# Layer 0's later modulations, moved from the chain stage to beneath the projection stage of a two-layer hybrid backbone

## Chip, cores and metric

One core of a Trainium2 chip. The metric is the time of one execution on the device in microseconds (us); for the kernel before it is the median of three runs. The engines are TensorE (PE; its weight loads are a row of their own, PEld), VectorE (DVE), ScalarE (ACT), GpSimd (POOL) and SyncE (SP), which only issues DMAs.

## What is computed

Two layers over 512 latent and 256 context tokens of width 1024, in fp32. Each sub-layer is norm, modulate, mixer, norm, gate, residual; the modulations are six vectors per layer, made from the conditioning vector by one large matrix:

```python
def ada_mod(cvec, w, b):
    m = jax.nn.silu(cvec) @ w + b            # (1024) @ (1024 x 6144)
    return six pieces of 1024                # shift, scale, gate; shift, scale, gate

for layer in range(2):
    ml, mc = ada_mod(c, ...), ada_mod(c_ctx, ...)
    hl = modulate(rmsnorm(xl), ml[0], ml[1]); hc = modulate(rmsnorm(xc), mc[0], mc[1])
    # layer 0: [spatial-gating MLP, 4 groups | bidirectional RWKV-7, 8 heads];  layer 1: mLSTM
    yl, yc = mixer(hl, hc)                   # layer 0: p = h @ w_in ... concat(...) @ w_out
    xl = xl + ml[2] * rmsnorm(yl)
    hl = modulate(rmsnorm(xl), ml[3], ml[4])
    xl = xl + ml[5] * rmsnorm(conv_ffn(hl))  # the same for the context with mc
```

Layer 0 needs pieces 0 and 1 before the projection, pieces 2 to 4 only after its mixer's output projection.

## The kernel before

All weights of the large products are split into a high and a low part, and each product is three matmuls (high by high, high by low, low by high). What matters here are two stages of layer 0.

**Projection stage** (about 60 to 372 us). `unit(col)` makes one tile of 128 output channels of `h @ w_in`: SP loads 512 KB into a buffer `raw_win` (line 115), ACT makes the high part (`hi_win`, line 124), POOL the low part (`lo_win`, line 125), and PE runs 24 matmuls over the 512 latent tokens (`pl_...`, lines 266 to 268) and 24 over the 256 context tokens (`pc_...`). There are two buffers each for raw, high and low, in the pool `wkR`. Three kinds of jobs use the results:
- `kr(ct)` and `v(ct)` make the tiles `kT`, `rT` and `vT` of RWKV's channel tile `ct` (0 to 3), with a convolution of three taps on ACT and DVE.
- `prep_e`, `prep_n` and `prep_t` prepare channel tile `ct` for the chains: small products from the low-rank inputs (`zw`, `za`, lines 504 to 506), the sets `RB` and `LB`, products of 64 x 64 (`nx`, `ny`, lines 565 and 566), and a blockwise triangular inverse whose steps go from PE (`w`, line 621, `t`, line 630) to DVE (`Td`, line 604) and ACT (`TT`, lines 613 and 614) and back. `Ts[0]` and `Ts[1]` are the inverses of channel tiles 2 and 3. The sets are stored to DRAM by SP (`setd`, lines 550 and 577).
- `sgu(g)` is spatial gate `g` (0 to 3): `unit` for `u`, `unit` for `v` (`vg`, ACT, line 813), and then in two parts (2 and 4 chunks of 128 tokens) transposes on PE (`vt`, line 822), a norm (`vn`), the product (`pz`, line 833) and its use on DVE.

Python generators hold these jobs, and `weave` merges them into one order: each entry is (generator, number of steps, offset), and at each step that generator goes on whose share of steps done is smallest, the share running from its offset to 1. `part_of(g, n)` runs n steps of a generator and leaves the rest. The tile scheduler keeps this order roughly and moves instructions by its own rules. `bank(name, "67")` takes the PSUM banks 6 and 7 in turn.

**Chain stage** (372 to about 616 us). The recurrences run in blocks b = 0 to 5 as chains (`c`, `y`, lines 708 to 743), woven with the preparation of the next block's operands (`lt`, line 653; `vt`, line 657; `az`, line 668; lines 621 and 630 still for `Ts`), and with the finished outputs. In blocks 2 to 4 the products of modulations 2 to 4 are woven in:

```python
            if b == 0:
                todo.append((chained(Ts[0], part_of(Ts[1], 6)), 14))
            elif b == 1:
                todo.append((inverse(), 9))
            elif b < 5:
                todo.append((part_of(ada, (5, 6, 5)[b - 2]), (5, 6, 5)[b - 2]))
```

`ada_gen(g, ...)` computes modulations 2 and 3 (g = 1) and 4 (g = 2). Over eight pieces of the contraction SP loads a slab of the matrix (line 154), and PE multiplies it with the two conditioning vectors; four 512-column pieces go to four 32-column quadrants of one bank (line 157, `32x512`). At the end there is a copy (`adasb`, line 162), four transposes (`adat`, line 165), and two sums into `mod`. In this kernel the slab has 2048 columns (1 MB) for g = 1 and 1024 (512 KB) for g = 2, in two buffers of the pool `late0`. Their first use is at the end of block 4.

Of the kernel before, what the change touches and what calls it, by code (L numbers as in the profile page):

```python
# [74 lines left out]
def _build(ctx, tc, xall, par, cst, ada_0, ada_w, ada_t, w_in, w_out, ffn_up, ffn_down, lora, wsT, a_bs, c_in, c_gate, c_out, mneg, parf, parm, out):  # L75
# [9 lines left out]
    def bank(name, role):  # L85

        turn[role] = turn.get(role, -1) + 1
        return pp.tile([P, 512], F32, tag=role[turn[role] % len(role)], name=name)
# [55 lines left out]
    def ada_gen(g, pool, tag, rawb, cols=1024, rtag="araw", width=None):  # L144

        n = min(2048, 5120 - g * 2048)
        width, cols = width or cols, min(cols, n)
        m = n // 512
        pb = bank(f"ada_{g}", tag)
        for kt in range(KT):  # L150
            for c0 in range(0, n, cols):
                pl = pool[(c0 // cols) % len(pool)] if isinstance(pool, list) else pool
                raw = pl.tile([P, width], F32, tag=rtag, name=f"ada{g}{kt}{c0}", bufs=rawb)[:, :cols]
                nc.sync.dma_start(raw, ada_w[kt, :, (g - 1) * 2048 + c0:(g - 1) * 2048 + c0 + cols])
                for q2 in range(cols // 512):
                    q = c0 // 512 + q2
                    nc.tensor.matmul(pb[32 * q:32 * q + 32, :], silu[:, kt, :],
                                     raw[:, q2 * 512:(q2 + 1) * 512],
                                     start=(kt == 0), stop=(kt == KT - 1))
            yield  # L160
        sb = (pool[0] if isinstance(pool, list) else pool).tile([P, width], F32, tag=rtag, name=f"adasb_{g}", bufs=rawb)[:, :512]
        V.tensor_copy(sb[:32 * m], pb[:32 * m])
        pt = bank(f"adat_{g}", tag)
        for j in range(4):
            nc.tensor.transpose(pt[:, j * 128:j * 128 + 32 * m], sb[:32 * m, j * 128:(j + 1) * 128], ident[:32 * m, :32 * m])

        o = PC.at["ada_b0"][0]
        for cnd in range(2):
            V.tensor_tensor(mod[0][:, cnd, g * 16:g * 16 + 4 * m].rearrange("p (q j) -> p q j", q=m),
                            pt.rearrange("p (j q r) -> p q j r", j=4, q=4)[:, :m, :, cnd],  # L170
                            par_s[:, o + g * 16:o + g * 16 + 4 * m].rearrange("p (q j) -> p q j", q=m), ALU.add)
# [130 lines left out]
    def weave(*gens):  # L302
        for _ in woven(*gens):
            pass

    def part_of(g, n):
        for _ in range(n):
            next(g)
            yield

    def run(gen):
        for _ in gen:
            pass
# [16 lines left out]
    with ExitStack() as lx:  # L330
# [471 lines left out]
                yield  # L802

        def sgu(g):
            role = "7" if g == 3 else "67"
            pl, pcx = unit(g, f"u{g}")
            ug = wkR.tile([P, T], F32, tag="ug", name=f"ug{g}", bufs=1)
            A.activation(ug[:, 0:TC], pcx, AF.Gelu_apprx_tanh)
            A.activation(ug[:, TC:T], pl, AF.Gelu_apprx_tanh)
            yield  # L810
            pl, pcx = unit(4 + g, f"vg{g}")
            vg = wkR.tile([P, T], F32, tag="vg", name=f"vg{g}", bufs=1)
            A.activation(vg[:, 0:TC], pcx, AF.Gelu_apprx_tanh)
            A.activation(vg[:, TC:T], pl, AF.Gelu_apprx_tanh)
            bsb = wkR.tile([P, P], F32, tag="bsb", name=f"bsb{g}")
            nc.sync.dma_start(bsb, a_bs[:, g * 128:g * 128 + 128].to_broadcast([P, P]))
            yield
            for (t0, nt) in ((0, 2), (2, 4)):
                pt = bank(f"vt{g}{t0}", role)
                for i in range(nt):  # L820
                    tk = t0 + i
                    nc.tensor.transpose(pt[:, i * 128:i * 128 + 128], vg[:, tk * 128:tk * 128 + 128], ident)
                ss = sm.tile([P, 4], F32, tag="ss4", name=f"sgss{g}{t0}", bufs=2)
                vn = wkR.tile([P, 512], F32, tag="vn", name=f"vn{g}{t0}", bufs=1)
                for i in range(nt):
                    A.activation(vn[:, i * 128:i * 128 + 128], pt[:, i * 128:i * 128 + 128], AF.Square, accum_out=ss[:, i:i + 1])
                G.tensor_scalar(ss[:, :nt], ss[:, :nt], 1.0 / 128, EPS, ALU.mult, ALU.add)
                G.tensor_tensor(ss[:, :nt], ss[:, :nt], eps_t[:, 2:3].to_broadcast([P, nt]), ALU.pow)
                V.tensor_tensor(vn[:, :nt * 128].rearrange("p (a q) -> p a q", q=128), pt[:, :nt * 128].rearrange("p (a q) -> p a q", q=128),
                                ss[:, :nt].unsqueeze(2).to_broadcast([P, nt, 128]), ALU.mult)  # L830
                pz = bank(f"pz{g}{t0}", role)
                for i in range(nt):
                    mm(pz[:, i * 128:i * 128 + 128], vn[:, i * 128:i * 128 + 128], wsT_s[:, g * 128:g * 128 + 128], start=True, stop=True)
                w = nt * 128
                o = vg[:, t0 * 128:t0 * 128 + w]
                ugs = ug[:, t0 * 128:t0 * 128 + w]
                V.scalar_tensor_tensor(o.rearrange("p (a q) -> p a q", q=128),
                                       pz[:, 0:w].rearrange("p (a q) -> p a q", q=128), pc("a_gv", g),
                                       bsb.unsqueeze(1).to_broadcast([P, nt, 128]),
                                       ALU.mult, ALU.add)  # L840
                V.tensor_tensor(o, o, ugs, ALU.mult)
                yield
            nc.sync.dma_start(mixd[g], vg)
# [15 lines left out]
        def chained(*gens):  # L859
            for g in gens:  # L860
                yield from g

        def start_prep(ct):
            PLt = keep.tile([P, 24], F32, name=f"PL{ct}")
            st[ct]["PL"] = PLt
            for k, n in SET:
                if k not in ("vT", "TT"):
                    st[ct][k] = wkS.tile([P, n], F32, tag=k, name=f"{k}{ct}")
            return prep_e(ct, st[ct]["kT"], st[ct]["rT"])
# [13 lines left out]
                yield  # L883

        NA = (4, 6, 6)
        Ts = [prep_t(ct, lambda name: bank(name, "7")) for ct in (2, 3)]
        run(kr(0))
        weave((start_prep(0), 8), (chained(v(0), kr(1), part(0)), 3 + 0))
        run(prep_n(0))
        for ct in range(3):  # L890
            n = NA[ct]
            weave((prep_t(ct, prbank), 13, 0.0) if ct < 2 else (part_of(Ts[0], 7), 7, 0.2), (chained(start_prep(ct + 1), prep_n(ct + 1)), 9 + 3, 0.0),
                  (chained(v(ct + 1), *([kr(ct + 2)] if ct < 2 else []), part(n)), 3 + n, 0.0))
        run(SG)
        ex.close()
        hx.close()
        rx.close()
# [49 lines left out]
            nc.sync.dma_start(t, set_part(ct, "bv"))  # L947
            st[ct]["bv"] = t

        late = {}  # L950

        def inverse():
            yield from Ts[1]
            tx.close()
            late["p"] = lx.enter_context(tc.tile_pool(name="late0", bufs=1))
            nc.scalar.dma_start(lwg, lora[:, 1024:1536])

        def preps(cts, g):
# [14 lines left out]
        for b, (k, g) in enumerate(blocks):  # L973
            n = (22, 20, 22 - 10 * k)[g]
            todo = [(part_of(C[k], n) if g < 2 or k else C[k], n)]
            if b < 5:
                kk_, gg_ = blocks[b + 1]
                todo.append((preps(pairs[kk_], gg_), 10))
            if b == 0:
                todo.append((chained(Ts[0], part_of(Ts[1], 6)), 14))  # L980
            elif b == 1:
                todo.append((inverse(), 9))
            elif b < 5:
                todo.append((part_of(ada, (5, 6, 5)[b - 2]), (5, 6, 5)[b - 2]))
            if b == 3:
                for ct in range(2):
                    load_bv(ct)
                todo.append((finish((0, 1), ys[0], ("01", "01"), "ctx"), 8))
            elif b == 4:
                todo.append((finish((0, 1), ys[0], ("01", "01"), "lat"), 8))  # L990
            elif b == 5:
                todo.append((finish((2, 3), ys[1], ("01", "01"), "ctx"), 8))
            weave(*todo)
            if g < 2:
                run(part_of(C[k], 4))
            if b == 1:
                ada = ada_job([1, 2], late["p"], 2, 2048)
            if b == 2:
                C.append(chains(pairs[1], ys[1]))
            if b == 4:  # L1000
                run(ada)
                gate_rows(0, 0, "7")
                scale_vec(0, 1)
                load_bv(2)
                load_bv(3)
# [606 lines left out]
```

## Time and profile before

| | us |
|---|---|
| median of 3 runs | 1954.63 (1948.76 to 1961.74) |
| the profiled execution | 1946.71 |
| its span, first to last instruction | 1944.9 |
| TensorE busy (12411 matmuls) | 1825.8 |
| VectorE busy | 1332.6 |
| ScalarE busy | 800.8 |
| GpSimd busy | 305.7 |
| mean granted TensorE clock | 0.97 of full |

Busy times are shares of one execution by the hardware profiler, and an engine's idle time is listed with what released it. The profiled execution is 0.4% below the median of the timed runs. Times within it, such as "372", are us from the start of its span.

### The profile page before, as it was taken

How to read it: one execution, taken by the hardware profiler on the slowest of the kernel's cores; microseconds unless marked ns; L12 is line 12 of the kernel's file. 1: busy time of each engine (PE TensorE's matmuls, PEld its weight loads, DVE VectorE, ACT ScalarE, POOL GpSimd, SP SyncE). 2: the span in 40 equal slices, each digit the busy share in tenths (PEclk: the TensorE clock that was granted, in tenths of full speed). 3: DMA queues.
4: the chain of work that ended last, by engine and by line, in shares of the span. 5: the costliest groups of instructions: out<-in, count | busy, mean ns of one | idle time of the engine just before them, and what ended most of it. 6: DMA issues, size and time to landing. Idle time of an engine off the chain costs nothing.

```text
span 1944.9 us, 31874 instructions
## 1 busy us (share of the span) xinstructions
PE 1825.8 (94%) x12411; PEld 1501.0 (77%) x12411; DVE 1332.6 (69%) x2669; ACT 800.8 (41%) x1429; POOL 305.7 (16%) x429
## 2 busy tenths in 40 slices
PE   6998789698998999999999998999999989999998
PEld 4777677587756888888888887778888768888886
DVE  4379676857445589999994337667777678777534
ACT  4374645524335542222232226575554343333322
POOL 2222222311000222323330002100110010000001
PEclk9999889889998999999999999999999999999999
DMA  7133121633774534444432224421111312222222
GB/s 296 55 125 125 67 96 65 194 83 93 221 201 137 173 106 158 152 168 163 163 136 77 101 96 163 159 86 44 33 44 44 130 68 98 97 96 95 93 97 87
DMA packets 102887, 227.77 MB, mean 117 GB/s; under 512 B 28224, under 2 KB 44048, under 8 KB 99664
## 3 DMA queue, kind: packets, MB, share of 16 engines
q1 hardware_dynamic: 100976, 222.26, 33.8%
q10 hardware_dynamic: 1760, 3.47, 0.5%
q8 instruction: 98, 1.61, 0.3%
q14 instruction: 53, 0.43, 0.1%
HBM read 199.31 MB, written 26.39 MB: 116 GB/s over the span
## 4 chain that ended last, share of the span: by engine, by line
PE 58%; DVE 2%; ACT 2%; POOL 1%; issue 1%; POOLq 0%; DVEq 0%; ACTq 0%
PE of L1044 5%; PE of L1045 5%; PE of L1043 5%; PE pl_fb L267 4%; PE pl_fb L268 4%; PE pl_fb L266 4%; PE pl_fa L267 4%; PE pl_fa L266 4%; PE pl_fa L268 4%; PE pd L1456 1%; PE pe L1433 1%; PE pc_fb L268 1%; PE pc_fa L268 1%; PE pc_fb L267 1%; PE pc_fa L267 1%; PE pc_fb L266 1%
## 5 line engine op out<-in xcount | busy, mean ns | idle before, releaser
L1091 DVE SCALAR_TENSOR_TENSOR cv<-pl_fa,fpar,cv 128x441 f32<-128x441 f32 (+2 forms) x352 | 243.2, 691 | 15.3 <-ACT cv L1080 10.0
L1045 PE MATMUL of<-hi_fd,hlo 128*128 128x512 f32 x440 | 171.4, 392 | 3.1 <-DVE hlo L1115 3.1
L1044 PE MATMUL of<-lo_fd,hhi 128*128 128x512 f32 x440 | 172.1, 391 | 1.6 <-DVE lo_fd L125 1.6
L1043 PE MATMUL of<-hi_fd,hhi 128*128 128x512 f32 x440 | 171.1, 391 | 0.0
L201 DVE SCALAR_TENSOR_TENSOR aj<-am,srb 128x512 f32<-128x512 f32 x224 | 163.4, 730 | 6.3 <-DMA am<-in_ada_t_dram 1.1
L1115 DVE TENSOR_TENSOR hlo<-hid,hhi 128x512 fp32r<-128x512 f32 (+1 forms) x66 | 39.1, 601 | 128.5 <-ACT hhi L1114 128.3
L1114 ACT ACTIVATE hhi<-hid 128x512 fp32r<-128x512 f32 (+1 forms) x66 | 36.7, 559 | 170.6 <-PE of L1044 167.2
L1045 PEld LDWEIGHTS of<-hi_fd,hlo 128*128 128x128 f32 x440 | 83.2, 189 | 20.7 <-DVE hlo L1115 3.5
L1044 PEld LDWEIGHTS of<-lo_fd,hhi 128*128 128x128 f32 x440 | 82.7, 188 | 19.9 <-DVE lo_fd L125 3.1
L125 DVE TENSOR_TENSOR lo_fd<-raw_fd,hi_fd 128x1024 fp32r<-128x1024 f32 x66 | 80.8, 1224 | 25.0 <-ACT hi_fd L124 24.9
L1043 PEld LDWEIGHTS of<-hi_fd,hhi 128*128 128x128 f32 x440 | 82.8, 188 | 17.9 <-DVE pt_f L1028 0.4
L222 POOL TENSOR_SCALAR rstd_p_f<-sq_f,sq_f 128x1 f32<-128x1 f32 x10 | 7.2, 724 | 557.2 <-ACT jk_f L1022 557.2
L124 ACT ACTIVATE hi_fd<-raw_fd 128x1024 fp32r<-128x1024 f32 x66 | 69.3, 1049 | 27.9 <-DMA raw_fd<-in_ffn_down_dram 11.8
L124 ACT ACTIVATE hi_fa<-raw_fa 128x1024 fp32r<-128x1024 f32 x44 | 46.4, 1055 | 76.3 <-PE pl_fb L267 62.7
L124 ACT ACTIVATE hi_fb<-raw_fb 128x1024 fp32r<-128x1024 f32 x44 | 46.7, 1062 | 68.2 <-PE pc_fa L267 39.0
L125 POOL TENSOR_TENSOR lo_fb<-raw_fb,hi_fb 128x1024 fp32r<-128x1024 f32 x22 | 59.4, 2698 | 88.9 <-ACT hi_fb L124 88.9
L125 POOL TENSOR_TENSOR lo_win<-raw_win,hi_win 128x1024 fp32r<-128x1024 f32 x23 | 57.6, 2508 | 91.2 <-ACT hi_win L124 85.0
L1093 ACT ACTIVATE cv<-cv 128x512 f32<-128x512 f32 x44 | 27.8, 632 | 106.4 <-DVE cv L1091 106.4
L266 PE MATMUL pl_fa<-h0f_lathi,hi_fa 128*128 128x512 f32 x176 | 69.0, 392 | 0.0
L266 PE MATMUL pl_fb<-h0f_lathi,hi_fb 128*128 128x512 f32 x176 | 68.8, 391 | 0.0
L267 PE MATMUL pl_fb<-h0f_latlo,hi_fb 128*128 128x512 f32 x176 | 68.8, 391 | 0.0
L267 PE MATMUL pl_fa<-h0f_latlo,hi_fa 128*128 128x512 f32 x176 | 68.8, 391 | 0.0
(695 smaller groups left out, 5485.5 us busy)
## 6 DMA issues: line engine op xcount, KB each, us to landing
raw_fd<-in_ffn_down_dram SPq DMA_DIRECT2D x66, 512.0 KB, 3.2
am<-in_ada_t_dram SPq DMA_DIRECT2D x112, 256.0 KB, 2.9
raw_fa<-in_ffn_up_dram SPq DMA_DIRECT2D x44, 512.0 KB, 3.3
raw_fb<-in_ffn_up_dram SPq DMA_DIRECT2D x44, 512.0 KB, 3.2
raw_win<-in_w_in_dram SPq DMA_DIRECT2D x23, 512.0 KB, 3.3
ada<-in_ada_dram SPq DMA_DIRECT2D x8, 1024.0 KB, 8.8
ada<-in_ada_w_dram SPq DMA_DIRECT2D x8, 1024.0 KB, 7.0
raw_cin<-in_c_in_dram SPq DMA_DIRECT2D x16, 512.0 KB, 3.5
```

The source lines that it names most:

```text
L124: nc.scalar.activation(hi[:, c], raw[:, c], AF.Copy)
L125: strm.sub.tensor_tensor(lo[:, c], raw[:, c], hi[:, c].bitcast(F32), ALU.subtract)
L201: V.scalar_tensor_tensor(place(f"aj{i}{h}{cnd}", "junk"), raw, 1.0, sb[cnd * 2 + h], ALU.mult, ALU.mult, accum_out=acc[:, cnd, h:h + 1])
L266: mm(p, wh[:, kt, :], hh[:, kt], start=(kt == 0), stop=False)
L267: mm(p, wh[:, kt, :], hl[:, kt], start=False, stop=False)
L268: mm(p, wl[:, kt, :], hh[:, kt], start=False, stop=(kt == KT - 1))
L1043: mm(o[i][hf], hi, w[0][:, c], start=f, stop=False)
L1044: mm(o[i][hf], hi, w[1][:, c], start=False, stop=False)
L1045: mm(o[i][hf], lo, w[0][:, c], start=False, stop=e)
L1091: V.scalar_tensor_tensor(dv, src[:, r0 + dy:r1 + dy, c0 + dx:c1 + dx], fw(ky * 3 + kx), dv, ALU.mult, ALU.add)
L1114: A.activation(hi, hid[cnd][:, k], AF.Copy)
L1115: V.tensor_tensor(lo, hid[cnd][:, k], hi.bitcast(F32), ALU.subtract)
```

## The change

The products of modulations 2 to 4 are no longer a job of the chain stage. `ada` is created ahead of the projection stage's weaves, with slabs of 1024 columns, in the two buffers with the tag `raw` that hold the raw projection weights, and with PSUM bank 7. Each of three weaves gets eight of its steps, and a step is now one load with its matmuls; the rest is run at the end. So there are 24 loads of 512 KB (two quadrants each) where there were 16 (eight of 1 MB, eight of 512 KB). The spatial gates use bank 6 alone. In the third weave the steps of `Ts[0]` get offset 0.0 and a count of 12 in place of 0.2 and 7. The pool `late0` and the steps in blocks 2 to 4 go.

```diff
                     nc.tensor.matmul(pb[32 * q:32 * q + 32, :], silu[:, kt, :],
                                      raw[:, q2 * 512:(q2 + 1) * 512],
                                      start=(kt == 0), stop=(kt == KT - 1))
-            yield
+                yield
...
         def sgu(g):
-            role = "7" if g == 3 else "67"
+            role = "6"
...
         NA = (4, 6, 6)
+        ada = ada_job([1, 2], wkR, strm.raw, 1024, "raw")
         Ts = [prep_t(ct, lambda name: bank(name, "7")) for ct in (2, 3)]
...
-            weave((prep_t(ct, prbank), 13, 0.0) if ct < 2 else (part_of(Ts[0], 7), 7, 0.2), (chained(start_prep(ct + 1), prep_n(ct + 1)), 9 + 3, 0.0),
+            weave((prep_t(ct, prbank), 13, 0.0) if ct < 2 else (part_of(Ts[0], 7), 12, 0.0), (part_of(ada, 8), 8, 0.0), (chained(start_prep(ct + 1), prep_n(ct + 1)), 9 + 3, 0.0),
                   (chained(v(ct + 1), *([kr(ct + 2)] if ct < 2 else []), part(n)), 3 + n, 0.0))
         run(SG)
+        run(ada)
...
-        late = {}
-
         def inverse():
             yield from Ts[1]
             tx.close()
-            late["p"] = lx.enter_context(tc.tile_pool(name="late0", bufs=1))
             nc.scalar.dma_start(lwg, lora[:, 1024:1536])
...
-            elif b < 5:
-                todo.append((part_of(ada, (5, 6, 5)[b - 2]), (5, 6, 5)[b - 2]))
...
-            if b == 1:
-                ada = ada_job([1, 2], late["p"], 2, 2048)
...
             if b == 4:
-                run(ada)
                 gate_rows(0, 0, "7")
```

What this does to the engines' queues shows at three places. In the rows below, a name is written `result<-operands`, with the number of its buffer behind it, then the shape and how many follow in a row.

SP's queue in the first third of the projection stage, before (`raw_win9` is the tile of column block 9; `setd0` and `setd1` are the stored sets of channel tiles 0 and 1):

```order
L115 DMA raw_win9_986<-in_w_in_dram 128x1024
L115 DMA raw_win17_1168<-in_w_in_dram 128x1024
L115 DMA raw_win14_1277<-in_w_in_dram 128x1024
L550 DMA setd0_583<-vT0_852 128x768
L115 DMA raw_win10_1362<-in_w_in_dram 128x1024
L577 DMA setd0_583<-RB0_778 128x3072
L577 DMA setd0_583<-LB0_779 128x3072
L550 DMA setd0_583<-bv0_780 128x768
L115 DMA raw_win0_1471<-in_w_in_dram 128x1024
```

and of the changed kernel from the same load (`ada100` is the slab of g = 1, piece 0, column 0):

```order
L115 DMA raw_win9_986<-in_w_in_dram 128x1024
L154 DMA ada100_1169<-in_ada_w_dram 128x1024
L115 DMA raw_win17_1173<-in_w_in_dram 128x1024
L550 DMA setd0_583<-vT0_852 128x768
L154 DMA ada101024_1268<-in_ada_w_dram 128x1024
L577 DMA setd0_583<-RB0_778 128x3072
L577 DMA setd0_583<-LB0_779 128x3072
L550 DMA setd0_583<-bv0_780 128x768
L115 DMA raw_win14_1286<-in_w_in_dram 128x1024
L154 DMA ada110_1362<-in_ada_w_dram 128x1024
```

Raw weights and slabs alternate, and the loads of column blocks 14 and later now stand behind the stores of channel tile 0.

PE's queue around the last spatial gate's first pass, `pl_u3`, before:

```order
L822 MATMUL vt20_2832<-cst_s_68,vg2_2646 128x128 x2
L266 MATMUL pl_u3_2930<-h0_lathi_104,hi_win3_2926 128x512
L267 MATMUL pl_u3_2930<-h0_latlo_105,hi_win3_2926 128x512
L504 MATMUL zwb3_1_2900<-twd_581,lw_569 128x256
L506 MATMUL zwa3_1_2902<-twd_581,lw_569 128x512
L504 MATMUL zab3_1_2907<-adt_582,lw_569 128x256
L506 MATMUL zaa3_1_2909<-adt_582,lw_569 128x512
L268 MATMUL pl_u3_2930<-h0_lathi_104,lo_win3_2927 128x512
```

and of the changed kernel at the same place:

```order
L822 MATMUL vt22_2967<-cst_s_68,vg2_2711 128x128 x4
L565 MATMUL nx31_3269<-RB3_2793,LB3_2794 64x64 x4
L566 MATMUL ny31_3270<-RB3_2793,LB3_2794 64x64 x4
L157 MATMUL ada_2_2897<-ada230_3097,silu_74 32x512
L833 MATMUL pz22_2981<-wsT_s_571,vn22_2973 128x128 x4
L157 MATMUL ada_2_2897<-ada230_3097,silu_74 32x512
L266 MATMUL pl_u3_3044<-h0_lathi_104,hi_win3_3040 128x512
```

The pass, which began among the pieces of the preparation (`zw`, `za`) and of the gate before it, now begins behind `vt22`, `nx31`, `ny31`, a group of the modulations and `pz22`.

PE's queue at the passage from the projection stage to the chain stage, before:

```order
L566 MATMUL ny32_3186<-RB3_2728,LB3_2729 64x64
L833 MATMUL pz32_3145<-wsT_s_571,vn32_3137 128x128 x4
L653 MATMUL lt000_3285<-cst_s_68,LB00_3262 128x128 x4
L657 MATMUL vt00_3297<-cst_s_68,v20_3258 128x128 x3
L653 MATMUL lt001_3291<-cst_s_68,LB00_3262 128x128 x4
```

and of the changed kernel:

```order
L157 MATMUL ada_2_2897<-ada270_3321,silu_74 32x512 x2
L833 MATMUL pz32_3262<-wsT_s_571,vn32_3254 128x128 x4
L165 MATMUL adat_2_3330<-cst_s_68,adasb_2_3328 128x64 x4
L621 MATMUL w20_3728<-TT2_3702,On2_3700 32x32 x32
L621 MATMUL w216_3788<-TT2_3702,On2_3700 32x32 x16
L630 MATMUL t20_3840<-Wm2_3727,Tn2_3697 32x32 x32
L653 MATMUL lt000_3401<-cst_s_68,LB00_3378 128x128 x4
```

Between the last gate's product and the first transpose of the chains there are now the transposes of g = 2 and the first matmuls of `Ts[0]`, which stood in block 0.

## The prediction

> **What bounds the kernel now.** I read the head of the page and its chain of work first, then busy time by windows cut at the stages, then TensorE's waits in the two stages that the change touches, then single tiles and lines.
>
> ```profile
> span 1944.9 us, 31874 instructions
> PE 58%; DVE 2%; ACT 2%; POOL 1%; issue 1%; POOLq 0%; DVEq 0%; ACTq 0%
> 60.00:150.00 90.00, 85.03 (x493) 67.88 (x492) 49.75 (x72) 50.00 (x79) 28.55 (x20) 0.96 0.29 103
> 150.00:200.00 50.00, 39.02 (x242) 32.34 (x240) 44.53 (x71) 23.73 (x30) 12.41 (x10) 0.90 0.30 111
> 200.00:276.00 76.00, 65.24 (x544) 53.14 (x542) 62.99 (x107) 39.45 (x75) 20.14 (x18) 0.93 0.26 99
> 276.00:340.00 64.00, 61.45 (x514) 49.87 (x515) 34.41 (x62) 37.72 (x79) 17.09 (x17) 0.87 0.15 54
> 340.00:372.00 32.00, 17.79 (x166) 14.59 (x164) 26.10 (x53) 18.11 (x42) 10.99 (x14) 0.87 0.52 186
> 490.00:582.00 92.00, 87.03 (x1340) 58.71 (x1339) 39.77 (x119) 33.25 (x83) 6.74 (x16) 1.00 0.72 214
> ```
>
> The second row is the chain that ended last: most of it is TensorE (PE). The others are windows in us from the span's start: length, busy time of PE, weight load, VectorE (DVE), ScalarE (ACT) and GpSimd (POOL), then the clock granted to TensorE, DMA share and GB/s. 60 to 372 is the projection stage, and 490 to 582 the blocks of the chain stage in which the modulations are computed today. There PE is busy 87.03 of 92 us at full clock: whatever is taken off PE there shortens the stage. The projection stage is mixed: in 150 to 276 DVE is nearly as full as PE (44.53 of 50, 62.99 of 76), in 276 to 340 PE is full (61.45 of 64), and in 340 to 372 PE has 14 us free.
>
> What PE waits for in the projection stage (line waiting, line released by; total us, times, longest):
>
> ```profile
> PE vt L822 <- ACT vg L813: 13.5, 2, 7.9
> PE lt L653 <- POOL AZ L916: 9.3, 1, 9.3
> PE pz L833 <- DVE vn L829: 5.3, 4, 2.1
> PE pl_rT L266 <- DVE kT L285: 5.1, 1, 5.1
> PE pl_rT L266 <- ACT a L518: 2.9, 1, 2.9
> ```
>
> These five make 36.1 us. None is a load of weights: the work there is late on DVE and ACT. And in 490 to 582:
>
> ```profile
> PE ada L157 <- DMA ada<-in_ada_w_dram: 2.4, 3, 1.2
> PE vt L657 <- ACT LT L654: 1.4, 2, 1.1
> PE az L668 <- ACT W L659: 0.3, 1, 0.3
> ```
>
> **What leaves the chain stage.** The line's group there, and one piece of eight records and one of four with the instruction behind it (start, duration):
>
> ```profile
> L157 PE MATMUL ada<-ada,silu 128*32 128x512 f32 x96 | 16.9, 605 | 2.4 <-DMA ada<-in_ada_w_dram 2.4
> 497.61 1.06 PE L157 MATMUL ada<-ada,silu 128*32 128x512 f32 x8
> 498.61 0.39 PE L739 MATMUL y<-AZ,W 128*64 128x64 f32 x6
> 578.09 1.05 PE L157 MATMUL ada<-ada,silu 128*32 128x512 f32 x4
> 579.07 0.45 PE L718 MATMUL c<-Qs,ttp 128*64 128x64 f32 x8
> ```
>
> The eight records work on four 32-column quadrants of the array side by side, the four on two; either way the next instruction starts 1.0 us later. So there are 16 groups of 1.0 us, 16.9 us busy in all, and the 2.4 us in which PE waited for their loads. The most that can go is 19.3 us. The least is about 5: the chains are recurrences (PE, DVE, ACT and back), and a group can stand in a gap that would come back as a wait. Since the other waits there make only 1.7 us, PE is held by its own work and I take a value near the upper end: **−15**.
>
> **What the moved inverse gives.** The first part of the third channel tile's inverse (lines 621 and 630) now stands ahead of the chain stage's first transposes, where PE waits 9.3 us for POOL; before it stood in block 0 (window and length, PE and weight load busy for that line's records alone, clock, DMA share, GB/s; line 621 first):
>
> ```profile
> 385.00:400.00 15.00, 2.98 (x86) 2.09 (x86) 1.00 0.59 163
> 385.00:410.00 25.00, 3.11 (x42) 2.16 (x42) 0.96 0.39 105
> ```
>
> Line 621 takes 2.98 us there and line 630 3.11. If all of it falls into the 9.3 us that PE idles, 6 us go; if it delays the padding on POOL or its transposes on DVE hold the chain's start, nothing. Only some of each is moved (48 of 86 and 32 of 42 records: 2.98 × 48/86 + 3.11 × 32/42 = 4 us) and PE's queue then stands ahead of the first chain transposes: **−2**.
>
> **What the projection stage takes on.** The same 96 matmuls now come as 24 groups of two quadrants (one load of 512 KB each), so 24 us of PE by the 1.0 us above. By the order of the changed program 13 groups stand ahead of passes or transposes that end in waits for DVE or ACT (150 to 276, where PE has 22 us free); 11 stand where PE is full or at the end. At worst all 24 lengthen the stage, at best none, since its waits make more than 24. Of the 11, the last four stand in the 14 us free after 340; so seven are uncovered: **+7**.
>
> The order on PE moves more than the groups. Three passes of the projection were fillers between pieces of the inverse and of the spatial gate, each waiting for another engine; here are the matmuls of `pl_vT` of channel tile 2 and of `pl_u` of gates 2 and 3 in those windows (window, length, busy, clock, DMA share, GB/s):
>
> ```profile
> 199.00:215.00 16.00, 4.37 (x11) 0.86 0.10 35
> 275.00:292.00 17.00, 8.04 (x24) 0.70 0.08 28
> 322.00:337.00 15.00, 7.57 (x24) 0.89 0.07 26
> ```
>
> The passes for `pl_u2` and `pl_u3` now stand as one piece behind the pieces that they filled, because their loads come later. If all filling is lost, 20 us of waits open; if other work steps in (ada groups do, one at a time), none. The waits of those pieces in the table are short (`pz` 2.1 at the longest), so I take a quarter: **+5**.
>
> Spatial gates now use one bank: the second half's transposes wait for DVE's read of the first half's product. And on ACT the gelu that makes `vg1` stands behind four copies of the inverse where it stood behind one:
>
> ```profile
> 193.16 1.52 ACT L613 COPY TT<-Td 32x768 f32<-32x768 f32 x1 [4.70 <-DVE Td L604]
> 199.21 0.38 ACT L813 ACTIVATE vg<-pc_vg 128x256 f32<-128x256 f32 x1
> ```
>
> Three more copies are 4.6 us, and they lengthen the 7.9 us wait for `vg`; the bank adds at most about 1 us at each of three gates. Between 0 and 7.5: **+3**.
>
> **Loads.** Each raw buffer now goes w_in, ada, w_in: a w_in load waits for an ada group on PE, and the ada load before it for the low part that POOL makes of the tile before. Durations min, median, max in ns, then start of the first and last; for loads the time to landing; SP's waits; and two matmuls of a pass that follow each other at full clock:
>
> ```profile
> L124 ACT ACTIVATE hi_win<-raw_win x23: 1041/1057/1077, 20.1 to 320.0; 128x1024 fp32r<-128x1024 f32 x23
> L125 POOL TENSOR_TENSOR lo_win<-raw_win,hi_win x23: 2346/2395/3190, 21.2 to 321.1; 128x1024 fp32r<-128x1024 f32 x23
> DMA to landing us min/median/max: 3.1/3.3/8.8
> SPq L115 <- POOL lo_win L125: 144.2, 15, 23.6
> SPq L577 <- DVE RB L537: 23.9, 3, 10.6
> 246.57 0.39 PE L266 MATMUL pl_rT<-h_lathi,hi_win 128*128 128x512 f32 x1
> 246.80 0.39 PE L267 MATMUL pl_rT<-h_latlo,hi_win 128*128 128x512 f32 x1
> L162 DVE COPY adasb<-ada x2: 683/688/692, 540.9 to 582.1; 128x512 f32<-128x512 f32 x1, 64x512 f32<-64x512 f32 x1
> ```
>
> Today the loads sit ready: SP waits 144.2 us in 15 waits for POOL to release a buffer, and PE never waits for a w_in load. After, a tile takes 3.3 to land, 1.06 for the high part and 2.4 for the low part, 6.8 us, and an ada load of the same size 3.3 ahead of it; the stores of line 577 in the same queue can hold both for up to 10.6 us. Behind a waiting ada load stand in SP's queue the next w_in load and the sets' stores; ACT's high part, and with it POOL's low part and PE's pass, wait for the one, and the next tile's RB and LB buffers for the other. Cover is the tile already split. The waits for landing are at least 0 and, with each of the 11 uncovered groups and its 3.3 us, at most 36. The nearest row is the 2.4 us that 16 loads cost in the chain stage: **+2**. Of DVE two copies of 0.7 us move along, with four small sums; DVE's queue has room behind 276 (34.41 of 64), so they cost nothing, and 1.4 us at most without that room.
>
> **Clock.** The granted clock is half in these stretches (same columns as the first windows; the last row sums seven such stretches):
>
> ```profile
> 196.50:203.30 6.80, 3.65 (x17) 2.82 (x18) 0.00 (x0) 6.64 (x14) 2.85 (x2) 0.50 0.00 0
> 237.50:244.30 6.80, 3.63 (x9) 2.89 (x10) 6.80 (x10) 3.46 (x7) 1.28 (x2) 0.50 0.23 77
> 364.00:381.00 17.00, 5.59 (x40) 4.85 (x41) 14.40 (x25) 8.61 (x9) 11.07 (x16) 0.51 0.92 230
> sum 54.10, PE 34.76 PEld 27.78 DVE 37.47 ACT 33.05 POOL 20.46; mean PE 4.97 PEld 3.97 DVE 5.35 ACT 4.72 POOL 2.92
> ```
>
> Each lies behind a wait: 7.9 us for `vg`, 5.1 for `kT`, 9.3 for `AZ`. PE is busy 34.76 us in them, and at full clock about half of that, 17 us, would go. Groups put into those waits can shorten them, and longer waits for `vg1` or `pl_u3` make new ones: between −17 and +5, and since one or two groups of 1.0 us in a wait of 8 leave it long, I take **−2**.
>
> The Trainium skill ("TensorE: Matmul & The Clock Gate", Part 1: The HAM clock gate) says that the clock falls to half after an idle window of some 3.4 us and comes back after as long a busy one. The rows agree: three waits of 5.1 us and more, each with 6.8 us or more at 0.50 behind or about it. By the rule the gain is all or nothing at each wait, which is the first rival's mechanism. The Trainium skill ("TensorEngine Tiling (Array Packing)", Key Properties) also says that a change of tiling mode drains TensorE. In the chain rows no such drain is seen beyond the 1.0 us between 128*32 and 128*64 neighbours; here the neighbours are whole-array matmuls, and no row of this case prices that for these groups. If each end of 24 groups cost one more step of 0.23 us as between the pass's matmuls, an estimate, the sum would be 11 us higher.
>
> **The sum.** −15 −2 +7 +5 +3 +2 −2 = −2 us. The profiled execution took 1946.7 us (span 1944.9); it would become 1944.7. The median of the three timed runs, 1954.63, stands 7.9 us above it; I carry that over: **1952.6**, told as 1952. A measurement of this kernel tells about 1%, 19.5 us, from no change.
>
> **Rivals.**
> - *The clock stays up.* The 13 early groups fall into the long waits and break them, so that PE returns at full clock: 8 of the 17 us go, the fillers' loss is none, and the chain stage gives the full 19.3. −19.3 −2 +3 (groups) +1 −8 = −25, 1930. For it: 13.5 us waiting for `vg` in two waits, just where groups stand. Against: a group stands ahead of the wait in PE's queue, so it shortens the wait's start and is not in its middle.
> - *All hidden, nothing else.* The groups cost nothing in 36 us of waits and the order nothing: −17, 1938. Against it: 276 to 340 is full.
> - *The loads come late.* The lead of w_in is one tile less. From the point where raw, ada, raw, with 6.8 + 3.3 us and SP's stores between, is longer than one unit's passes (24 matmuls of 512 columns, 0.23 us apart, are 5.5 us, and 24 of 256 half of that: 8.3 us), each unit waits. Five units (`pl_vT2`, `vg1`, `pl_u2`, `vg2`, `pl_u3`) by 4 us of landing and split, and half as long again at half clock, are +30; with the groups' +7 and −16 from the chain stage +21, 1975: slower. For it: 10.1 us against 8.3, and stores that wait 10.6. Against: between passes PE does the inverse, and in 312 us 23 tiles need 13.6 us each.
> - *The change does not do what it says*, if the chain stage's pieces took as long without the groups: then only the +15 of the projection stage is left, 1970. Its 87.03 of 92 speak against it.
>
> **How the numbers follow.** Forecast 0.60 (own range 1942 to 1965: each of the terms off by about half); clock 0.12; hidden 0.10; late loads 0.13; no gain in the chain stage 0.05. The range of 1932 to 1973 holds the forecast, the hidden and the last case, and leaves out half and more of the first and third rival, and a few hundredths at the forecast's ends. Faster by over 1% (below 1935): most of the clock case and a little of the hidden one, 0.13. Slower by over 1% (above 1974): most of the late loads and a little of the others, 0.11. Between: 0.76.
>
> **What would show it.** In the changed profile: (1) chain stage shorter by 13 to 21 us from its first transpose to the output projection, with PE's waits there no longer than before; (2) 24 ada groups of about 1 us in the projection stage; (3) that stage longer by 8 to 20; (4) PE's wait for `vg` about as long or up to 5 longer; (5) waits of PE for w_in's low or high part near 2 us in all; rows of 10 or more are the third rival; (6) half-clock stretches between 45 and 60 us in sum; under 40 is the first rival; (7) from the output projection on the same. I am wrong if the projection stage grows by more than 25 or not at all.

## The result: 0.7% faster, and the profile after

The changed kernel takes 1938.7 us in the median of four runs (1937.66 to 1940.08), the one before 1953.3 beside it: ratio 0.9928, 95% interval 0.9906 to 0.9951. Timed again in another set it was 0.9944 (0.9927 to 0.9961). So 11 to 14 us are gained. The prediction was 1952, a gain of 2, in a range of 1932 to 1973 that holds the result.

Windows of the two stages, cut at the first transpose and the last product of the chains (window, length, busy PE, weight load, DVE, ACT, POOL, clock, DMA share, GB/s). Before, two executions:

```profile
60.00:372.40 312.40, 268.53 (x1950) 217.82 (x1948) 218.19 (x362) 169.41 (x303) 89.55 (x79) 0.92 0.28 102
372.40:606.80 234.40, 216.37 (x3655) 167.19 (x3657) 129.00 (x379) 88.05 (x209) 28.00 (x58) 0.93 0.50 141
```

```profile
60.00:375.50 315.50, 270.17 (x1949) 219.09 (x1948) 216.99 (x361) 169.32 (x303) 91.19 (x79) 0.90 0.28 101
375.50:610.50 235.00, 216.53 (x3656) 167.47 (x3657) 128.93 (x379) 87.99 (x209) 27.82 (x58) 0.93 0.51 140
```

and the changed kernel, two executions as well:

```profile
60.00:395.00 335.00, 295.61 (x2214) 220.99 (x2212) 229.76 (x380) 173.23 (x306) 98.00 (x87) 0.94 0.39 136
395.00:597.30 202.30, 187.17 (x3397) 155.03 (x3393) 120.77 (x360) 82.58 (x203) 22.68 (x51) 0.93 0.35 95
```

```profile
60.00:400.00 340.00, 299.59 (x2218) 224.16 (x2218) 230.94 (x386) 173.67 (x307) 98.08 (x87) 0.93 0.40 134
400.00:602.30 202.30, 187.12 (x3397) 154.97 (x3393) 120.82 (x360) 82.52 (x203) 22.50 (x51) 0.93 0.35 95
```

The chain stage is 32.1 us shorter (234.4 to 202.3; PE's busy time 216.37 to 187.17), the projection stage 22.6 us longer between the first profiles (312.4 to 335.0) and 24.5 between the second ones. A part of both is work of the inverse that changed sides of the cut: of line 621 the profile has 192 matmul records ahead of it before and 288 after, of line 630 192 and 256, and these take 5.4 us more there. What follows is unchanged: from the first output-projection matmul to the last one of the kernel 1320.2 us before and 1320.6 after.

PE's waits in the changed projection stage:

```profile
PE vt L822 <- ACT vg L813: 9.9, 2, 5.7
PE w L621 <- ACT TT L614: 6.5, 2, 3.7
PE pl_rT L266 <- DVE kT L285: 5.9, 2, 3.0
PE pz L833 <- DVE vn L829: 4.8, 6, 1.8
PE pl_vg L266 <- ACT ug L809: 3.6, 2, 3.2
```

The wait for `vg` is 3.6 us shorter. The 9.3 us ahead of the chains are gone from the list; in their place PE waits 6.5 us for `TT` and 2.1 for `Wm` of the moved inverse. The place of the old 5.1 us wait for `kT` shows what groups do to a wait (start, duration):

```profile
236.50 1.05 PE L157 MATMUL ada<-ada,silu 128*32 128x512 f32 x4
237.93 1.05 PE L157 MATMUL ada<-ada,silu 128*32 128x512 f32 x2 [0.38 <-DMA ada<-in_ada_w_dram]
241.98 0.77 PE L266 MATMUL pl_rT<-h_lathi,hi_win 128*128 128x512 f32 x1 [3.01 <-DVE kT L285]
```

Groups stand in the first 2.5 us, and 3.0 are left. Work ahead of a wait shortens it too: the last matmul of gate 1's `vg` started at 190.4 us before and at 193.7 after, but ACT's gelu behind it at 199.2 and 199.7, so that wait fell from 7.9 to 4.2 us.

### The profile page after: what moved, and what is told of

It is laid out like the page before. It is cut to its first block, busy times and chain, and to the rows that moved or that the text cites. A ratio compares the mean times of both kernels' runs of the same rounds, so it can differ in the third digit from the quotient of the medians.

```text
span 1935.7 us, 31912 instructions
## 1 busy us (share of the span) xinstructions
PE 1824.3 (94%) x12411; PEld 1492.2 (77%) x12411; DVE 1335.3 (69%) x2669; ACT 798.8 (41%) x1427; POOL 309.3 (16%) x429
## 4 chain that ended last, share of the span: by engine, by line
PE 57%; DVE 2%; ACT 2%; POOL 2%; DMA 1%; issue 1%; POOLq 0%; DVEq 0%; ACTq 0%; SPq 0%
PE of L1038 5%; PE of L1037 5%; PE of L1039 5%; PE pl_fb L268 4%; PE pl_fb L266 4%; PE pl_fb L267 4%; PE pl_fa L267 4%; PE pl_fa L266 4%; PE pl_fa L268 4%; PE pd L1450 1%; PE pe L1427 1%; PE pc_fb L268 1%; PE pc_fa L268 1%; PE pc_fb L267 1%; PE pc_fa L267 1%; PE pc_fb L266 1%
```

## The experiments

All ratios are to the kernel before, timed in the same set.

**The products left out, in both places.** Before, the steps in blocks 2 to 4 go; after, the entry of the weaves. In both, `mod` is filled with the bias:

```diff
-                todo.append((part_of(ada, (5, 6, 5)[b - 2]), (5, 6, 5)[b - 2]))
+                pass
...
+                    V.tensor_copy(mod[0][:, cnd, 16:40], par_s[:, o + 16:o + 40])
```

> The kernel before with the products of modulations 2 to 4 left out of the chain stage (the modulations there are their bias alone; loads, matmuls and transposes are gone, nothing is added elsewhere). Theory 1, the chain stage is bound by PE and pays for every group: its 15.9 us of groups, 1.0 us of transposes and 2.4 us of landing waits go, 19 to 22 us in all, so about 0.989 to 0.990 of before. Theory 2, the gain seen in the changed kernel's chain stage beyond that comes from the clock: only 10 us or so go here, 0.995, or over 25 us, by chance of the stretch at half clock.

> The changed kernel with the same products left out (modulations 2 to 4 are their bias alone), all else as in it: offset of the inverse and one bank for the gates kept. Theory 1, the groups cost the projection stage nearly what they cost the chain stage: it is 15 to 24 us below the changed kernel, about 0.981 to 0.985 of before, and its projection stage ends 15 to 24 us before that of the changed kernel. Theory 2, the waits of the projection stage hide the groups: within 5 us of the changed kernel, 0.990 to 0.993.

Measured: 0.9874 (0.9854 to 0.9895), 24.6 us of 1954, and 0.9850 (0.9829 to 0.9871), 29.3 us. The job costs the kernel before 24.6 us and the changed kernel 0.9928 − 0.9850 = 0.8% or 0.9944 − 0.9850 = 0.9%, 15 to 18 us. Moving it is worth 6 to 9 us, where each ratio is known to 0.2%, 4 us. In the changed kernel that is within the 15 to 24 us of theory 1; the kernel before paid more than theory 1's 19 to 22 us and just under the 25 that theory 2 lays to chance. The chain stage without it:

```profile
377.10:589.80 212.70, 200.33 (x3551) 165.00 (x3553) 125.68 (x368) 86.62 (x209) 27.09 (x57) 0.92 0.36 95
```

PE's busy time falls by 16.0 us (216.37 to 200.33) and its idle time by 5.7 (18.0 to 12.4), 21.7 in all, where only 2.4 of idle were named as waits for loads. Most of the other 3.3 are shorter waits for `LT` (1.4 us), `TT` and `ttp` (0.8 each) and `W` (0.3), less 0.5 of longer ones. The remaining 3 us lie within the spread of executions.

And the changed kernel's projection stage without the groups:

```profile
60.00:383.90 323.90, 277.07 (x2013) 223.75 (x2012) 222.28 (x367) 172.32 (x304) 93.76 (x83) 0.88 0.28 100
```

Beside it the groups' own row from the lines of the changed kernel:

```profile
L157 PE MATMUL ada<-ada,silu 128*32 128x512 f32 x96 | 30.0, 639 | 1.6 <-DMA ada<-in_ada_w_dram 1.3 <-PE zab L504 0.3
```

They are 30.0 us busy, where the chain stage's were 16.9: there are 24 groups in place of 16, each as long with two quadrants as with four, and some run at half clock (mean 639 ns a record against 605). The stage grew by 11.1 us (323.9 to 335.0), and by 16.1 to the second execution of the changed kernel (340.0), although it also holds 32 more records of line 621 and 64 more of line 630. PE's idle time fell by 7.4 us (46.8 to 39.4, and to 40.4 in the second execution), and all other matmuls together took less: the clock was 0.88 without the groups and 0.94 and 0.93 with them.

**The half clock.** Sums over the stretches in which at most 0.53 was granted, from 60 us to the end of the projection stage: before; the changed kernel, twice; it without the groups:

```profile
sum 52.90, PE 36.56 PEld 27.72 DVE 31.37 ACT 28.96 POOL 18.47; mean PE 4.57 PEld 3.46 DVE 3.92 ACT 3.62 POOL 2.31
```

```profile
sum 41.50, PE 31.77 PEld 21.67 DVE 20.53 ACT 18.45 POOL 20.98; mean PE 4.54 PEld 3.10 DVE 2.93 ACT 2.64 POOL 3.00
```

```profile
sum 45.00, PE 38.64 PEld 27.05 DVE 22.29 ACT 17.18 POOL 25.38; mean PE 4.83 PEld 3.38 DVE 2.79 ACT 2.15 POOL 3.17
```

```profile
sum 75.40, PE 55.00 PEld 40.84 DVE 44.44 ACT 35.14 POOL 22.47; mean PE 5.50 PEld 4.08 DVE 4.44 ACT 3.51 POOL 2.25
```

With groups 42 and 45 us, without them 75: PE had 16 to 23 us less of work at half clock, half of which, 8 to 12 us, is time won back. That and the 6 to 7 us of idle time are what the groups hide in. The 75 us are of one execution, but the two kinds do not overlap in any profile of these runs: without groups the stage had 53 to 79 us at half clock (seven executions of six kernels), with eight groups in each weave 36 to 47 (four executions of three). Against the kernel before the gain is smaller: PE's work at half clock there was 36.6 us, and 41.0 in its second profile, against 31.8 and 38.6.

**The loads left out, the groups kept.**

```diff
-                raw = pl.tile([P, width], F32, tag=rtag, name=f"ada{g}{kt}{c0}", bufs=rawb)[:, :cols]
-                nc.sync.dma_start(raw, ada_w[kt, :, ...])
...
-                                     raw[:, q2 * 512:(q2 + 1) * 512],
+                                     cst_s[:, 0:512],
```

> The changed kernel with the 24 loads of the slabs left out: the same 96 matmuls in the same weaves read a constant that lies in SBUF, so that the raw buffers belong to the projection weights alone again (modulations 2 to 4 are meaningless). Theory 1, what the groups cost the projection stage is their time on PE, less what they take from waits and from stretches at half clock: within 4 us of the changed kernel, 0.991 to 0.994 of before. Theory 2, the loads through the shared buffers are the greater part of the 12 to 13 us that the groups cost there: 7 us or more below the changed kernel, 0.989 or less.

Measured: 0.9899 (0.9881 to 0.9916), 0.3 to 0.45% below the changed kernel: 6 to 9 us. It lies between the theories, nearer to the second. Of the 15 to 18 us that the job costs the changed kernel, 9.6 are the groups (0.9899 − 0.9850, to some 4 us) and the rest the loads through the shared buffers. The projection stage without the loads:

```profile
60.00:387.90 327.90, 289.53 (x2218) 217.34 (x2218) 229.72 (x385) 174.88 (x309) 95.64 (x85) 0.95 0.28 100
```

It is 7.1 us shorter than in the first profile of the changed kernel and 12.1 than in the second. PE's idle time is only 1.0 and 2.0 us less; its busy time is 6.1 and 10.1 us less, and 36 us are at half clock in which PE is busy 21.0 us, 11 and 18 less than with the loads. So most of what the loads cost is work at half clock and not a wait for a load.

**The inverse, alone and put back.**

```diff
-(part_of(Ts[0], 7), 7, 0.2)
+(part_of(Ts[0], 7), 12, 0.0)
```

> The kernel before with one number changed, the steps of the third channel tile's inverse in the third weave with offset 0.0 and count 12. Theory 1, that is a move of 5 to 7 us of PE work from block 0 into the 9.3 us in which PE waits ahead of the chains: 2 to 5 us faster, 0.997 to 0.999. Theory 2, it explains most of the gain: 0.994 or less. Theory 3, it only delays the chains' start: 1.000 or above.

> The changed kernel with offset and count of that inverse as before (0.2 and 7). Theory 1: 2 to 5 us above the changed kernel, 0.994 to 0.996 of before. Theory 2, the inverse is most of the gain: 0.998 to 1.000. Theory 3: at the changed kernel's 0.993 or below.

Alone: 0.9977 (0.9961 to 0.9992), 4.5 us, as theory 1 says. Put back: 0.9942 (0.9923 to 0.9961), between the changed kernel's two results, so no difference is shown.

**One bank alone.**

```diff
-            role = "7" if g == 3 else "67"
+            role = "6"
```

> The kernel before with one number changed, the spatial gates in PSUM bank 6 alone. Theory 1, the second part's transposes wait for the read of the first part's product, 0 to 3 us: 1.000 to 1.0015. Theory 2, with a bank of their own the gates meet the inverses less, which use bank 7: 2 us or more faster, 0.999 or less, and then part of the changed kernel's gain is the bank's.

Measured: 0.9968 (0.9952 to 0.9985), 6.3 us faster; theory 1 is wrong, and the size is that of theory 2. Its one profile, at 1949.8 us, does not show the gain: it is above the first profile of before, with 79 us at half clock in the projection stage. Matmul records of line 621 ahead of the chains (window, busy and number of that line's alone), of before, one bank alone, the inverse alone, the inverse put back and the changed kernel:

```profile
60.00:372.40 312.40, 3.79 (x192) 3.34 (x192) 0.92 0.28 102
```

```profile
60.00:385.30 325.30, 6.66 (x274) 5.90 (x274) 0.88 0.28 100
```

```profile
60.00:378.10 318.10, 5.87 (x256) 5.29 (x256) 0.90 0.28 102
```

```profile
60.00:400.20 340.20, 7.23 (x288) 6.30 (x288) 0.93 0.40 134
```

```profile
60.00:395.00 335.00, 7.23 (x288) 6.30 (x288) 0.94 0.39 136
```

Each of the two edits alone brings parts of the inverse ahead of the chains (192 to 274 and to 256 records), and together, without the groups, they gave no more than one (0.9850 against 0.9874, 4.7 us, and each known to 0.2%). That they are two ways to the same gain is argued from this; no run changes the bank and keeps the order. With the offset put back, 288 stand ahead of the chains all the same, which fits that run's showing no difference.

**Where the slabs stand.**

```diff
-(part_of(ada, 8), 8, 0.0)
+(part_of(ada, (4, 8, 12)[ct]), (4, 8, 12)[ct], 0.0)     # and (6, 8, 10); for two weaves 12, 12 and no entry
```

> The changed kernel with 12 slabs in each of the first two weaves and none in the third, where PE has the fewest waits. Theory 1, groups cost least where DVE and ACT hold PE up: 3 to 8 us below the changed kernel, 0.989 to 0.991 of before. Theory 2, the loads of w_in are then later in the first two weaves and PE waits for them: 3 us or more above the changed kernel, 0.994 or more. Theory 3, place does not matter: 0.992 to 0.993.

> The changed kernel with 4, 8 and 12 slabs in the three weaves in place of 8, 8 and 8. Theory 1, an early slab holds back the loads of w_in (with 12, 12 and 0 the kernel was 15 us slower than the changed one), so later is better: 2 to 6 us below the changed kernel, 0.990 to 0.992 of before. Theory 2, the groups are cheap where they fall into waits that would bring TensorE to half clock, and the third weave has fewest of these: 2 to 8 us above the changed kernel, 0.994 to 0.997.

> The changed kernel with 6, 8 and 10 slabs in the three weaves. Half of the step to 4, 8 and 12, in the same direction: theory 1 0.991 to 0.993, theory 2 0.993 to 0.995.

Measured: two weaves 1.0006 (0.9994 to 1.0018), all the gain lost; 4, 8, 12 0.9954 (0.9938 to 0.9971); 6, 8, 10 0.9975 (0.9958 to 0.9993). In the same set 8, 8, 8 had 0.9944, so 4, 8, 12 is not told from it, and 6, 8, 10 is slower by 6.7 us in the median. With two weaves these waits are new or longer, the first of them for weights:

```profile
PE pl_u L266 <- ACT hi_win L124: 4.8, 1, 4.8
PE bon1b L453 <- DVE bv L546: 4.1, 1, 4.1
PE pl_u L266 <- DVE vT L285: 3.6, 1, 3.6
```

Its projection stage, and the sum over its stretches at half clock:

```profile
60.00:411.40 351.40, 307.61 (x2214) 232.21 (x2212) 227.13 (x379) 174.01 (x306) 91.61 (x83) 0.90 0.37 128
sum 70.90, PE 58.98 PEld 42.54 DVE 43.10 ACT 32.68 POOL 23.38; mean PE 6.55 PEld 4.73 DVE 4.79 ACT 3.63 POOL 2.60
```

The projection stage is 16.4 us longer than in the first profile of the changed kernel and 11.4 than in the second. Waits for a high or low part make 8.0 us (4.8 for the high part, 3.2 for low ones) where they made 0.3; PE's idle time is 4.4 us more and its busy time 12.0, with 71 us at half clock in place of 42. So the third rival's wait comes when slabs crowd, below its 10 us, and slow matmuls make the larger part. 6, 8, 10 fits neither theory: a step of two slabs costs 0.3%, the step of four beyond it nothing that shows. The profile of 6, 8, 10 has 56 us at half clock and that of 4, 8, 12 has 59; what of the loss is clock and what loads was not separated.

**Narrow slabs in the chain stage, and a second look at before.**

```diff
-                ada = ada_job([1, 2], late["p"], 2, 2048)
+                ada = ada_job([1, 2], late["p"], 4, 1024)     # with a step per load, 8 in each block
```

> The kernel before with the slabs as in the changed one, 24 of 512 KB, in four buffers of the old pool, with eight steps in each of blocks 2 to 4: 24 groups of two quadrants in place of 16. Theory 1, a group costs 1.0 us of PE whatever its number of quadrants: 6 to 9 us slower, 1.003 to 1.005. Theory 2, the form and the landing waits are what was costly in the chain stage: no slower, 0.997 to 1.001. It bears on what the 25 us are that leaving the products out of the chain stage gave, where 19 are accounted for.

> The kernel before once more, unchanged, for a second profile: its timed executions lie between 1945.6 and 1960.7 and the first profile's was 1946.7, near the lower end. If its time is above 1951, theory 1: the difference to the first profile lies in the chain stage, in its groups, their landing waits and stretches at half clock, 4 us or more of it. Theory 2: it is spread over the later stages, and the chain stage is within 2 us.

Narrow slabs: 1.0020 (1.0008 to 1.0033), 3.9 us slower, less than the 8 us of eight more groups at 1.0 us. Its chain stage was 4.9 us longer (239.3). PE's busy time rose by 8.5 us, as theory 1 says (216.37 to 224.91), and its idle time fell by 3.6. So fewer quadrants to a group do not make the job cheaper there.

The second look took 1950.5, just under the 1951 that the theories name, and neither fits: the chain stage is as long (235.0 against 234.4), the later stages too, and the 3.1 us are in the projection stage (372.4 to 375.5). That stage ran unchanged in two more kernels, to 377.1 and 381.7. The first profile was the earliest of four, and the spread goes with the clock: 312.4, 315.5, 317.1 and 321.7 us of length go with 53, 63, 60 and 70 us at half clock.

**The changed kernel once more.**

> The changed kernel once more, for a second profile and a closer interval: 0.991 to 0.995 of before. Theory 1, its stages end within 3 us of those of its first profile (first transposes of the chains at 395.0, chain stage 202.2 us long), and the stretches at half clock in the projection stage are below 50 us. Theory 2, the first profile was by chance a good one, and these spread by 10 us as those of the kernel before do (372.4 to 381.7 where the same projection stage ran).

Measured: 0.9944 (0.9927 to 0.9961). The chain stage is again 202.3 us and half clock 45 us, but the first transposes come at 400.0 in place of 395.0: half of theory 2's spread of 10, and theory 1 as to the clock.

## Why the prediction held in its range but not in its size

The job's price in the projection stage, +7 +5 +2 −2 = +12 without the bank, was not far from the 15 to 18 us measured. The steps that failed are on the other side: −15 for the chain stage was −24.6, and −2 for the inverse with the bank's cost in +3 was −4.7. Both windows moved further than the prediction's signs allowed, 32.1 us against 13 to 21 and 22.6 to 24.5 against 8 to 20, in part by the moved inverse. The range held by its width of 41 us and the right direction. The rival *All hidden* names 1938, where the kernel took 1938.7, by chance: it has the groups cost nothing, and the job costs 15 to 18 us.

1. *Chain stage, −15.* It was 24.6 us by leaving the job out. The step that failed is the upper end of 19.3: it added busy time and the waits laid to the loads, and 5.7 us of idle time went instead of 2.4, the rest in short waits for `LT`, `TT`, `ttp` and `W`.
2. *The moved inverse, −2.* The direction was right, the size was −4.5 alone. The sum's share, 48 of 86 and 32 of 42, sets matmuls of the program against records of the profile, and each of these matmuls leaves two records: 96 and 64 records moved, 5.4 us of PE and not 4. The bank, in +3 as a cost, is a gain of 6.3 alone. Together they are worth 4.7, with some 4 us of uncertainty, since each of the two ratios behind it is known to 0.2%.
3. *Seven uncovered groups, +7; lost filling, +5; bank and ACT's order, +3.* The three were to give +15 with the groups. By the runs the groups cost 9.6. The wait for `vg` did not grow by 4.6 but fell by 3.6: a group stands at its start, PE comes to it later, and no lengthening by ACT's copies is seen.
4. *Landing waits, +2.* The waits themselves are small (1.3 us for slabs, 0.3 for a low part of w_in), but leaving the loads out gave 6 to 9 us, most of it work at half clock. ACT does come to wait: 11.9 us in three waits for a raw tile to land, where it had none.
5. *Clock, −2.* Against the kernel before, half of the work at half clock that went is between a gain of 5 us and a loss of 1, depending on the two profiles compared; −2 lies within. Against the same kernel without groups it is 8 to 12 us. That is the first rival's mechanism, and its 8 us, but only against a kernel that its other two edits had brought to 75 us at half clock; its 3 us for the groups did not come in.
6. *The 7.9 us carried over* from the profiled execution to the median do not hold for the changed kernel, whose first profile (1937.7) and median differ by 1.0 us. Between the first profiled executions the gain was 9.0 us and between the second ones 8.2 (1950.5 to 1942.3), between the medians 14.6 and 12.0. Both profiles of before lie below its median; its slower executions were not seen in a profile.

So −24.6 (out of the chain stage) −4.7 (inverse and bank) +9.6 (groups) +6 to 9 (loads) = −14 to −11. The sum has to come out, since its terms are differences of the same ratios; what it tells is the size of each.

The stretches at half clock, 3.5, 7.0, 10.5 and 14 us when read in windows of 0.5 us, are multiples of one length. The Trainium skill ("TensorE: Matmul & The Clock Gate", Part 1: The HAM clock gate) gives its window as some 3.4 us. The trace agrees. The Trainium skill ("TensorEngine Tiling (Array Packing)", Key Properties) also names a drain at a change of tiling mode. The prediction's estimate of 11 us for it at whole-array neighbours did not come: at full clock the next instruction starts 1.0 us behind a group of four records whether it is a whole-array matmul (274.09 to 275.07 us in the changed kernel), one of 64 x 64 (193.87 to 194.86) or one of 128 x 64 in the chain stage. What a drain takes within that 1.0 us is not shown.

## What to carry to other kernels

An engine that holds a dense stage up can be worth relieving even when the receiving stage pays much of it back: here 24.6 us were taken out and 15 to 18 paid. What made it less were waits in the receiving stage, and the matmuls at half clock behind them. So count a wait of TensorE with the slow matmuls behind it, and profile the kernel twice before a median is worked out from one execution. Loads through shared buffers can cost without a wait for any of them, so test how they are spread: 8, 8, 8 and 4, 8, 12 were alike here, 12, 12 lost all the gain. And count in one unit: a matmul of the program can be two records of the profile.

## What the runs showed of the hardware

The stretches at half clock come in steps of 3.5 us, or 3.41 by the profile's own times of the changes: behind the same wait for `kT` it was 7.0 us in one execution of the changed kernel and 3.5 in the other, and from execution to execution of one program the projection stage's end moved by 5 us (395.0 and 400.0).

```profile
241.50:245.00 3.50, 3.02 (x7) 2.44 (x8) 3.46 (x7) 1.79 (x2) 0.40 (x1) 0.52 0.00 0
```

```profile
243.00:250.00 7.00, 6.28 (x15) 4.97 (x16) 6.86 (x10) 1.79 (x2) 2.49 (x2) 0.51 0.08 7
```

What stands ahead of a stretch shows when the projection stages of all 14 profiles are cut at these steps of 3.41 us. Behind a window at full clock in which PE was busy for less than 1.5 us the clock was half in all 79 cases; with 1.5 to 2.5 us in 30 of 77; with more in 12 of 957, ten of these 12 with 64 to 128 records of the inverse's 32 x 32 matmuls. Another 33 busy windows with 60 or more of these did not lose the clock. By these counts a group of 1.0 us in a wait can lift a window out of the first kind; which groups did so was not followed one by one.

In the chain stage both kernels have a stretch at half clock of 17 to 20 us among the small matmuls of the inverse, where no wait is longer than 2.6 us. The window ahead of it shows the same two kinds: in the changed kernel (466.7 to 470.2 us) PE is busy 0.85 us, between waits for `TT`; before (404.7 to 408.1) it is busy throughout, 2.2 us of it with 36 records of line 630. That these matmuls cause it was not tried.
